# A decoder in float32r on one core: a weight tile's first part multiplied with both parts of x in one 512-column matmul

## The chip, the core and the metric

One of the cores of a Trainium2 chip runs the whole program. The metric is the device time of one execution in microseconds (us), the median of three runs. The engines are named as in the profile: PE is TensorE's matmuls, PEld its weight loads, DVE is VectorE, ACT is ScalarE, POOL is GpSimd, and SP issues DMAs.

## The reference, cut to what matters

256 tokens of width 1024 pass through five blocks in turn. Each has the same frame: a norm, weight matrices, a residual add.

```python
x = x + 0.5 * swiglu(rmsnorm(x, ff1_norm), w_gate, w_up, w_down)      # FF1, 1024 -> 2816 -> 1024
proj = rmsnorm(x, mix_norm) @ w_in                                    # mixer: 7168 columns
...                                                                   # gates, gMLP branch, stick-breaking attention
x = x + (g_a * (y_a @ w_branch_a) + g_b * (y_b @ w_branch_b)) @ w_out
x = x + 0.5 * swiglu(rmsnorm(x, ff2_norm), w_gate, w_up, w_down)      # FF2
h = rmsnorm(x, final_norm)                                            # the second network starts here
h = h + moba_attention(q, k, v) @ w_o_2[0];  h = h + relu(n(h) @ w_up)**2 @ w_down   # MLP a, 1024 -> 4096 -> 1024
h = h + forgetting_attention(q, k, v, c) @ w_o_2[1];  h = h + relu(n(h) @ w_up)**2 @ w_down   # MLP b
out = rmsnorm(h, final_norm_2)
```

All inputs are float32, and every weight element is used once for the 256 tokens.

## The kernel before, in words

**Split arithmetic.** A float32 product is made of three float32r matmuls. A weight W is split into a first part `whi` (W rounded to float32r, one ACT copy, line 130) and a rest `wlo` = W - `whi` (one DVE subtraction, line 137). The activations are split in the same way into `hnh` and `hnl`. The product is `whi·hnh + whi·hnl + wlo·hnh`.

**Stream of weights.** Weights come by DMA in 403 pieces of 128 x 1024 elements, called halves (`raw`, 6 buffers). Work is written out in units, mostly one half each. In unit u ACT splits half u+3 and DVE half u+2 (5 buffers of `whi`, 4 of `wlo`), then PE multiplies half u. A half holds 8 tiles of 128 x 128, so a unit is 24 matmuls. The loop at the end of the program sets the order of everything: for each unit the functions registered with `pre`, the two splits, those registered with `mid`, the unit's matmuls, and those registered with `at`. Each engine works through its own instructions in that order.

**Groups.** A `Group` is a pass over all rows of K for up to 1024 columns. The transposed output goes to PSUM: 128 columns of the weight on the partitions, 256 tokens along the bank, two such tiles to a bank of 512. A group of 1024 columns fills the four banks of one ring, "A" or "B", and the next group takes the other ring. After a group, DVE reads each bank with its next operation (times `rstd`, or the residual add), so there is no separate copy. Three kinds of groups work in another way: `v`, the mixer's `gv` and the last projection are token-major, with x as the stationary operand and 512 columns of weight moving.

**Norms.** `norm_at(u, ...)` is written into the first units of a block: sums of squares of x (ACT squares, DVE sums into `acc`), a matmul of `ones` with `acc` on PE (function `c`, at the end of unit u+3), a square root on ACT and a reciprocal on DVE (function `d`). The factor is applied when a group's banks are read, which is after 8 units.

**Residuals.** `resid` adds banks to `xT` on DVE and splits the new x for the next block: ACT writes the first part of each k-tile, DVE the rest. For two banks together it issues both adds, then the four first parts, then the four rests.

Of the kernel before, what the change touches and what calls it, by code (L numbers as in the profile page):

```python
# [15 lines left out]
D = 1024  # L16
# [10 lines left out]
class Group:  # L27
    """One pass over K of a weight matrix's columns, accumulating in two or four PSUM banks."""

    def __init__(self, ring, srcs, ktiles, xin, tok=False, stagger=0):  # L30
        self.ring, self.srcs, self.ktiles, self.xin = ring, srcs, ktiles, xin
        self.tok, self.stagger = tok, stagger
# [7 lines left out]
def decoder_kernel(  # L40
# [18 lines left out]
    psum = ctx.enter_context(tc.tile_pool(name="psum", bufs=4, space=bass.MemoryType.PSUM))  # L59
# [7 lines left out]

    def bank(ring):
        return psum.tile([128, 512], F32, name=f"ps{ring}", tag=f"ps{ring}")
# [10 lines left out]
    # ---------------------------------------------------------------- weight stream  # L80
# [59 lines left out]
    def unit_mm(u):  # L140
        g, hs = units[u]
        if g.ps is None:
            g.ps = [bank(g.ring) for _ in range(g.banks)]
            g.started = [False] * g.banks
# [6 lines left out]
        def ws(h, kl, b, parts=(0, 1, 2)):  # L151
            k = halves[h][1] + kl
            last = k == g.ktiles - 1
            for j in range(2):
# [3 lines left out]
                xh, xl = g.xin(k, nt)  # L158
                dst = g.ps[b][:, j * T:(j + 1) * T]
                for i in parts:  # L160
                    mm(b, dst, wl if i == 2 else wh, xl if i == 1 else xh, last and j == 1 and i == 2)

        def tsm(h, kl, tok, chs):
# [3 lines left out]
            xh, xl = g.xin(k, 0)  # L167
            xh, xl = xh[:, tok * 128:(tok + 1) * 128], xl[:, tok * 128:(tok + 1) * 128]
# [34 lines left out]
    # ---------------------------------------------------------------- constants  # L203
# [86 lines left out]
    # ---------------------------------------------------------------- norms  # L290
    def hn_tiles():
        return (big.tile([128, 8, T], F32R, name="hnh", tag="hnh"),
                big.tile([128, 8, T], F32R, name="hnl", tag="hnl"))

    def scaled(dst, src, cols, k):
        """dst = (hi, lo) of src times the per-partition gain; src is x^T's k-tile."""
        hh, hl = dst
        S.activation(hh[:, k, :], src, AF.Copy, scale=cols[:, k:k + 1])
        V.scalar_tensor_tensor(hl[:, k, :], src, cols[:, k:k + 1], raw32(hh[:, k, :]),
                               op0=OP.mult, op1=OP.subtract)  # L300
# [5 lines left out]
    def resid(g, alpha, outs, banks):  # L306
        """x^T += alpha * psum, then its scaled splits for the next layer."""
        for b in banks:
            xb = xT[:, 2 * b:2 * b + 2, :]
            V.scalar_tensor_tensor(xb, v2(g.ps[b]), alpha, xb, op0=OP.mult, op1=OP.add)  # L310
            for k in (2 * b, 2 * b + 1):
                for (hh, _), cols in outs:
                    S.activation(hh[:, k, :], xT[:, k, :], AF.Copy, scale=cols[:, k:k + 1])
        for b in banks:
            for k in (2 * b, 2 * b + 1):
                for (hh, hl), cols in outs:
                    V.scalar_tensor_tensor(hl[:, k, :], xT[:, k, :], cols[:, k:k + 1], raw32(hh[:, k, :]),
                                           op0=OP.mult, op1=OP.subtract)
# [3 lines left out]
    def squares(cols=None):  # L322
        sq = []
        for b in range(4):
# [10 lines left out]
    def add_up(acc, sq):  # L335
        V.tensor_add(sq[0], sq[0], sq[1])
        V.tensor_add(sq[2], sq[2], sq[3])
        V.tensor_add(sq[0], sq[0], sq[2])
        V.tensor_add(acc, sq[0][:, :T], sq[0][:, T:])

    def norm_at(u, ring, two=False, cols=False):
# [3 lines left out]
        def a():  # L345
            R.clear()
            R["sq"] = squares()
            R["acc"] = smalls.tile([128, 2, T], F32, name="acc", tag="acc", bufs=1)

        def b():  # L350
            add_up(R["acc"][:, 0, :], R["sq"])
            if two:
                R["sq"] = squares(gcol[:, G_FIN:G_FIN + 8])

        def b2():
            add_up(R["acc"][:, 1, :], R["sq"])

        def c():
            p = bank(ring)
            R["p"] = p  # L360
            PE.matmul(p[:, :n], ones, R["acc"].rearrange("p a t -> p (a t)")[:, :n], start=True, stop=True)
# [10 lines left out]
        def d2():  # L372
            """1 / sqrt(s2 / D + eps * (s1 / D + eps)): both norms' factors at once."""
            r = smalls.tile([128, T], F32, name="rstd2", tag="rstd", bufs=2)
            S.activation(r, R["p"][:, :T], AF.Copy, scale=EPS)
            V.tensor_add(r, r, R["p"][:, T:])
# [16 lines left out]
        def f():  # L393
            r = R["bc"]
            p = bank(ring)
# [5 lines left out]

        pre(u + 1, a)
        pre(u + 2, b)
        if two:
            pre(u + 3, b2)
        v = u + 4 if two else u + 3
# [14 lines left out]
    # ---------------------------------------------------------------- layers  # L421
# [3 lines left out]
    def hn_in(k, nt):  # L425
        return cur["hn"][0][:, k, :], cur["hn"][1][:, k, :]

    def fixed_in(name):
        def f(k, nt):
            h, l = cur[name]  # L430
            assert (id(h), k) in ready, (name, k)
            return h[k // 8][:, k % 8, :], l[k // 8][:, k % 8, :]
        return f
# [3 lines left out]
    def hidden(name, his, los):  # L437
        def mk():
            cur[name] = ([slot(i, [128, 8, T], F32R, name=name + "h") for i in his],
                         [slot(i, [128, 8, T], F32R, name=name + "l") for i in los])  # L440
        return mk

    def hid(name, nt):
        h, l = cur[name]
        return h[nt // 8][:, nt % 8:nt % 8 + 2, :], l[nt // 8][:, nt % 8:nt % 8 + 2, :]

    def put_hidden(u, name, nt, src, fin=None):
        """The split of two column tiles, its first part in unit u and its second in the next."""
        hv, lv = hid(name, nt)

        def lo():
            V.tensor_sub(lv, src, raw32(hv))
            ready.update((id(cur[name][0]), nt + j) for j in range(2))

        S.activation(hv, src, AF.Copy)
        pre(u + 1, lo)

    def swiglu_evac(u, g, n0, bg, bu, name):
        r = bc2(R["bc"])
        t, w = temp(name="gt"), temp(name="ut")  # L460
        tv, uv = v2(t[:, :512]), v2(w[:, :512])
        V.tensor_mul(tv, v2(g.ps[bg]), r)
        V.tensor_mul(uv, v2(g.ps[bu]), r)
        S.activation(tv, tv, AF.Silu)

        def b():
            V.tensor_mul(uv, uv, tv)
            put_hidden(u + 1, name, n0, uv)

        pre(u + 1, b)  # L470

    def ffn(ring, name, wg, wu, wd, his, los):
        other = {A: B, B: A}
        r, first = ring, None
        for i in range(6):
            c0 = 512 * i
            w = min(512, DFF - c0)
            g = add(Group(r, [(wg, c0, w), (wu, c0, w)], 8, hn_in))
            if first is None:
                first = g  # L480
                at(g.u0, hidden(name, his, los))
                norm_at(g.u0 or 2, other[r])
            nb = g.banks // 2
            for b in range(nb):
                at(g.u1 + b, swiglu_evac, g.u1 + b, g, 4 * i + 2 * b, b, nb + b, name)
            r = other[r]
        return add(Group(r, [(wd, 0, D)], DFF // 128, fixed_in(name), stagger=2))

    # start: x^T and its split
    g1, u1, d1 = ff1_w_gate[0], ff1_w_up[0], ff1_w_down[0]  # L490
    ff1 = ffn(A, "ffa", g1, u1, d1, (1, 2, 3), (4, 5, 6))

    def resid_to(g, alpha, bases):
        def f():
            outs = []
            cur["hn"] = hn_tiles()
            outs.append((cur["hn"], bases[0]()))
            if len(bases) > 1:
                cur["hn2"] = (slot(6, [128, 8, T], F32R, name="kvh"), slot(7, [128, 8, T], F32R, name="kvl"))
                outs.append((cur["hn2"], bases[1]()))  # L500
            resid(g, alpha, outs, (0, 1))
            at(g.u1 + 1, resid, g, alpha, outs, (2, 3))
        at(g.u1, f)
# [3 lines left out]
    # ---- mixer  # L507
    win = w_in[0]
    gates = [add(Group((B, A)[i], [(win, 5120 + i * D, D)], 8, hn_in)) for i in range(2)]
    norm_at(gates[0].u0, A, cols=True)  # L510
    at(gates[0].u0 + 1, late_consts)
    at(gates[0].u0 + 1, w_s_prep, A)
# [9 lines left out]
    def gate_evac(g, i, b):  # L522
        if b == 0:
            cur["gate", i] = slot((0, 7)[i], [128, 8, T], name="gate")
        t = temp(name="gl")
        V.tensor_mul(v2(t[:, :512]), v2(g.ps[b]), bc2(R["bc"]))
        for j in range(2):
            nt = 2 * b + j
# [669 lines left out]
```

## Time and profile before

| | |
|---|---|
| time, median of 3 runs | 1259.06 us (1258.83 to 1259.13) |
| profiled execution: span from its first to its last instruction | 1257.2 us |
| the same execution's own time | no separate figure is given; the median of the runs lies 1.9 us above the span |
| PE busy | 1247.9 us, 9770 instructions |
| DVE busy | 827.1 us |
| ACT busy | 663.5 us |
| mean granted clock of TensorE | 0.999 |
| DMA | 217.68 MB, mean 173 GB/s |

Busy time of an engine is the time in which at least one of its instructions is under way. Matmuls overlap in the pipeline, so what a matmul costs is read from the distance between the starts of two, not from its duration.

### The profile page before, as it was taken

To read this page: it belongs to the slowest core of one execution; us is meant where nothing else is said; L and a number is where in the kernel's file an instruction comes from. 1 tells how busy PE (TensorE), PEld (TensorE's weight loads), DVE (VectorE), ACT (ScalarE), POOL (GpSimd) and SP (SyncE) were. 2 spreads that over 40 slices of the span, in tenths; PEclk is the share of its full clock that TensorE was granted. 3 is DMA by queue.
4 is the path that set the end of the run, shared out by engine and by line. 5 is a ranking of instruction groups with operands and counts; after the bars stand their busy time and mean duration, and the time that the engine had idled before them with its cause. 6 is when DMAs were issued, how large, how long until landed. Compare 5 with 4: busy or idle time off the path is not lost.

```text
span 1257.2 us, 23928 instructions
## 1 busy us (share of the span) xinstructions
PE 1247.9 (99%) x9770; PEld 1197.9 (95%) x9770; DVE 827.1 (66%) x1226; ACT 663.5 (53%) x945; POOL 2.7 (0%) x7
## 2 busy tenths in 40 slices
PE   9999999999999999999999999999999999999997
PEld 8999999999989999999999899999999989999886
DVE  6765647658667676667568777755448677856644
ACT  6543436554666455444356655655336656655433
POOL 0000000000000000000000000000000000000000
PEclk9999999999999999999999999999999999999999
DMA  8665555755444456565555445655553434555661
GB/s 280 194 209 175 188 184 171 220 178 153 154 147 140 155 185 195 166 202 179 190 157 163 135 141 183 190 190 184 180 183 130 153 129 138 192 186 175 209 193 49
DMA packets 100095, 217.68 MB, mean 173 GB/s; under 512 B 10041, under 2 KB 39825, under 8 KB 99985
## 3 DMA queue, kind: packets, MB, share of 16 engines
q1 hardware_dynamic: 99408, 214.32, 53.1%
q10 hardware_dynamic: 576, 1.84, 0.4%
q8 instruction: 76, 1.25, 0.4%
q14 instruction: 35, 0.28, 0.1%
HBM read 215.07 MB, written 1.05 MB: 172 GB/s over the span
## 4 chain that ended last, share of the span: by engine, by line
PE 99%; DMA 0%; DVE 0%; SPq 0%; issue 0%; ACT 0%; POOL 0%; POOLq 0%
PE psB L148 49%; PE psA L148 43%; PE psB L693 1%; PE psB L673 1%; PE psA L693 1%; PE psA L735 0%; PE psA L673 0%; DMA xin<-in_x_dram 0%; PE psB L979 0%; PE psA L581 0%; PE psB L677 0%; PE psB L842 0%; PE psB L844 0%; PE psB L843 0%; PE psA L737 0%; PE psB L808 0%
## 5 line engine op out<-in xcount | busy, mean ns | idle before, releaser
L137 DVE TENSOR_TENSOR wlo<-raw,whi 128x1024 fp32r<-128x1024 f32 x403 | 488.2, 1221 | 243.9 <-PE psB L148 112.5
L130 ACT ACTIVATE whi<-raw 128x1024 fp32r<-128x1024 f32 x403 | 417.7, 1052 | 287.9 <-PE psB L148 171.2
L148 PE MATMUL psA<-hnh,whi 128*128 128x256 f32 x928 | 263.7, 286 | 0.0
L148 PE MATMUL psA<-hnh,wlo 128*128 128x256 f32 x928 | 261.4, 283 | 0.0
L148 PE MATMUL psA<-hnl,whi 128*128 128x256 f32 x928 | 261.2, 283 | 0.0
L148 PE MATMUL psB<-hnh,whi 128*128 128x256 f32 x800 | 228.1, 285 | 0.0
L148 PE MATMUL psB<-hnh,wlo 128*128 128x256 f32 x800 | 226.4, 283 | 0.0
L148 PE MATMUL psB<-hnl,whi 128*128 128x256 f32 x800 | 226.3, 283 | 0.0
L148 PEld LDWEIGHTS psA<-hnh,whi 128*128 128x128 f32 x928 | 177.4, 192 | 1.5 <-issue 1.1
L148 PEld LDWEIGHTS psA<-hnl,whi 128*128 128x128 f32 x928 | 177.5, 192 | 0.4 <-issue 0.2
L148 PEld LDWEIGHTS psA<-hnh,wlo 128*128 128x128 f32 x928 | 177.4, 192 | 0.2 <-DVE wlo L137 0.2
L148 PEld LDWEIGHTS psB<-hnh,whi 128*128 128x128 f32 x800 | 153.5, 192 | 0.5 <-issue 0.3
L148 PEld LDWEIGHTS psB<-hnl,whi 128*128 128x128 f32 x800 | 153.5, 192 | 0.1
L148 PEld LDWEIGHTS psB<-hnh,wlo 128*128 128x128 f32 x800 | 153.5, 192 | 0.0
L148 PE MATMUL psB<-mah,whi 128*128 128x256 f32 x256 | 72.4, 283 | 0.0
L148 PE MATMUL psB<-mal,whi 128*128 128x256 f32 x256 | 72.4, 283 | 0.0
L148 PE MATMUL psB<-mah,wlo 128*128 128x256 f32 x256 | 72.4, 283 | 0.0
L148 PE MATMUL psB<-whi,mbh 128*128 128x512 f32 x128 | 49.9, 390 | 0.0
L148 PE MATMUL psB<-wlo,mbh 128*128 128x512 f32 x128 | 49.8, 389 | 0.0
L148 PE MATMUL psA<-ffah,whi 128*128 128x256 f32 x176 | 49.8, 283 | 0.0
L148 PE MATMUL psA<-ffal,whi 128*128 128x256 f32 x176 | 49.8, 283 | 0.0
L148 PE MATMUL psA<-ffah,wlo 128*128 128x256 f32 x176 | 49.8, 283 | 0.0
(305 smaller groups left out, 2264.9 us busy)
## 6 DMA issues: line engine op xcount, KB each, us to landing
raw<-in_w_up_dram SPq DMA_DIRECT2D x64, 512.0 KB, 4.2
raw<-in_w_down_dram SPq DMA_DIRECT2D x64, 512.0 KB, 3.5
raw<-in_ff_w_gate_dram SPq DMA_DIRECT2D x88, 256.0 KB, 3.2
raw<-in_ff_w_up_dram SPq DMA_DIRECT2D x88, 256.0 KB, 4.2
raw<-in_ff_w_down_dram SPq DMA_DIRECT2D x44, 512.0 KB, 4.0
raw<-in_w_in_dram SPq DMA_DIRECT2D x40, 512.0 KB, 4.2
raw<-in_w_in_dram SPq DMA_DIRECT2D x32, 256.0 KB, 3.0
raw<-in_moba_w_qkv_dram SPq DMA_DIRECT2D x32, 256.0 KB, 3.0
```

The costliest lines, as they stand in the source:

```text
L130: S.activation(hi_t[h], raw_t[h].rearrange("p k c -> p (k c)"), AF.Copy)
L137: V.tensor_sub(lo_t[h], raw_t.pop(h).rearrange("p k c -> p (k c)"), raw32(hi_t[h]))
L148: PE.matmul(dst, lhsT, rhs, start=not g.started[b], stop=stop, skip_group_check=True)
L673: PE.matmul(O[64 * h:64 * h + 64, 0:256], vv[:, 0, c:c + 64], w[:, h * 384:h * 384 + 256], start=True, stop=False, skip_group_check=True)
L693: PE.matmul(banks[h][:, c:c + n], left[i][rw, cl:cl + 128], right[j][rw, cr:cr + n], start=start and i + j == 0, stop=i == 1, skip_group_c ...
```

## The change

A group may now be `wide`. In a wide group a bank belongs to one tile of 128 columns. Its left half (256 tokens) takes `wlo·xh` and `whi·xh`, its right half takes `whi·xl`. Since the two parts of x lie next to each other now (one tile `[128, k, 2, T]` in place of two tiles), `whi` meets both in one matmul of 512 columns. Reading needs the sum of the two halves: `gather` copies the right halves of two banks to SBUF on ACT and adds the left halves on DVE. A wide group has 512 columns, so it is 4 units and not 8. Wide are the two feed-forward blocks, the gates, `u`, `w_out`, and both MLPs with their down projections except the last one: 2080 tiles, of which the first 16 run in three matmuls of 256 columns, as before.

With this go: PSUM tiles of two banks (`banks2`, two to a ring), the norm's functions one unit earlier (`c` at the end of unit u+2) and in two halves, `resid` one pair of banks at a time, and the attention biases of MoBA made at the start of FF2 and not in its down projection.

```diff
-        self.banks = self.width // 256
+        self.banks = self.width // (128 if wide else 256)
...
-    psum = ctx.enter_context(tc.tile_pool(name="psum", bufs=4, space=bass.MemoryType.PSUM))
+    psum = ctx.enter_context(tc.tile_pool(name="psum", bufs=2, space=bass.MemoryType.PSUM))
...
+            if g.wide:
+                col = kl * g.width + b * 128
+                wh, wl = hi_t[h][:, col:col + 128], lo_t[h][:, col:col + 128]
+                x = g.xin(k, b)
+                if len(parts) == 3:
+                    mm(b, g.ps[b][:, :T], wl, x[:, 0, :], False)
+                    mm(b, g.ps[b], wh, both(x), last)
...
+    def gather(g, p, name="gs"):
+
+        t = v2(temp(name=name)[:, :512])
+        S.activation(t, g.pairs[p][:, :, T:], AF.Copy)
+        V.tensor_add(t, g.pairs[p][:, :, :T], t)
+        return t
+
+    def resid(g, p, n0, alpha, outs):
+
+        xb = xT[:, n0:n0 + 2, :]
+        if g.wide:
+            t = v2(temp(name="rs")[:, :512])
+            S.activation(t, g.pairs[p][:, :, T:], AF.Copy)
+            V.scalar_tensor_tensor(xb, t, alpha, xb, op0=OP.mult, op1=OP.add)
+            src = g.pairs[p][:, :, :T]
+        else:
+            src = v2(g.ps[p])
+        V.scalar_tensor_tensor(xb, src, alpha, xb, op0=OP.mult, op1=OP.add)
+        for k in (n0, n0 + 1):
+            for ts, cols in outs:
+                S.activation(part(ts, k, 0), xT[:, k, :], AF.Copy, scale=cols[:, k:k + 1])
+        for k in (n0, n0 + 1):
+            for ts, cols in outs:
+                V.scalar_tensor_tensor(part(ts, k, 1), xT[:, k, :], cols[:, k:k + 1], raw32(part(ts, k, 0)),
+                                       op0=OP.mult, op1=OP.subtract)
...
-        pre(u + 1, a)
-        pre(u + 2, b)
-        if two:
-            pre(u + 3, b2)
-        v = u + 4 if two else u + 3
+        pre(u if u0 is None else u0, a0)
+        pre(u + 1, a1)
+        mid(u + 1, b)
+        v = u + 3 if two else u + 2
         at(v, c)
...
-        for i in range(4):
-            g = add(Group(r, [(w, D * i, D)], 8, hn_in))
+        for i in range(8):
+            g = add(Group(r, [(w, 512 * i, 512)], 8, hn_in, wide=True))
...
+            def evac(g=g, i=i, p=0):
+                tv = gather(g, p, "rl")
+                V.scalar_tensor_tensor(tv, tv, 0.0, bc2(R["bc"]), op0=OP.max, op1=OP.mult)
                 S.activation(tv, tv, AF.Square)
-                pre(g.u1 + b + 1, put_hidden, g.u1 + b + 1, name, 8 * i + 2 * b, tv)
+                pre(g.u1 + p + 1, put_hidden, g.u1 + p + 1, name, 4 * i + 2 * p, tv)
...
+    def down(r, w, ktiles, xin, stagger=2):
+
+        return [add(Group((r, flip(r))[i], [(w, 512 * i, 512)], ktiles, xin, stagger=i * stagger, wide=True))
+                for i in range(2)]
...
-        at(ff2.u0 + 1 + h, moba_bias, h)
+        at(ff2[0].u0 - 43 + h, moba_bias, h)
```

**PE, two weight tiles in FF1.** Before, three matmuls of 256 columns to a tile:

```order
L148 MATMUL psB<-hnh,whi 128x256
L148 MATMUL psB<-hnl,whi 128x256
L148 MATMUL psB<-hnh,wlo 128x256
L148 MATMUL psB<-hnh,whi 128x256
L148 MATMUL psB<-hnl,whi 128x256
L148 MATMUL psB<-hnh,wlo 128x256
```

and now, three tiles of the same block (`hn` holds both parts of x):

```order
L161 MATMUL psB<-hn,wlo 128x256
L161 MATMUL psB<-hn,whi 128x512
L161 MATMUL psB<-hn,wlo 128x256
L161 MATMUL psB<-hn,whi 128x512
L161 MATMUL psB<-hn,wlo 128x256
L161 MATMUL psB<-hn,whi 128x512
```

The matmul with `wlo` stands first now, and the one with `hnl` is gone as an instruction of its own.

**DVE at the start of MLP a.** `xT` rows are residual adds, `hnl` (now `hn`) the rests of the split x, `sq` and `acc` the norm's sums, `wlo` the splits of the weight stream, `rstd` the reciprocal. Before:

```order
L137 TENSOR_TENSOR wlo<-raw,whi 128x1024
L310 SCALAR_TENSOR_TENSOR xT<-psA,xT 128x512 x2
L317 SCALAR_TENSOR_TENSOR hnl<-xT,gcol,hnh 128x256 x4
L137 TENSOR_TENSOR wlo<-raw,whi 128x1024
L336 TENSOR_TENSOR sq<-sq 128x512
L337 TENSOR_TENSOR sq<-sq 128x512
L338 TENSOR_TENSOR sq<-sq 128x512
L339 TENSOR_TENSOR acc<-sq 128x256
L137 TENSOR_TENSOR wlo<-raw,whi 128x1024 x2
L368 RECIPROCAL rstd<-rstd 128x256
```

and now, from the first sum of squares on:

```order
L383 TENSOR_TENSOR sq<-sq 128x512
L149 TENSOR_TENSOR wlo<-raw,whi 128x1024
L348 SCALAR_TENSOR_TENSOR xT<-psA,xT 128x512
L354 SCALAR_TENSOR_TENSOR hn<-xT,gcol,hn 128x256 x2
L348 SCALAR_TENSOR_TENSOR xT<-psA,xT 128x512
L354 SCALAR_TENSOR_TENSOR hn<-xT,gcol,hn 128x256 x2
L149 TENSOR_TENSOR wlo<-raw,whi 128x1024
L391 TENSOR_TENSOR sq<-sq 128x512
L392 TENSOR_TENSOR sq<-sq 128x512
L393 TENSOR_TENSOR acc<-sq 128x256
L149 TENSOR_TENSOR wlo<-raw,whi 128x1024
L405 RECIPROCAL rstd<-rstd 128x256
```

Each add is now followed by its own two rests, one sum has moved ahead of the second pair of adds, and between `acc` and the reciprocal stands one `wlo` and not two.

**DVE between two groups of MLP a.** `rl` is the tile that holds relu of the group's columns, `mal` (now `ma`) the rest of the hidden activations. Before:

```order
L892 SCALAR_TENSOR_TENSOR rl<-psB,rstd 128x512
L137 TENSOR_TENSOR wlo<-raw,whi 128x1024
L892 SCALAR_TENSOR_TENSOR rl<-psB,rstd 128x512
L452 TENSOR_TENSOR mal_8935<-rl,mah_8931 128x512
L137 TENSOR_TENSOR wlo<-raw,whi 128x1024
L892 SCALAR_TENSOR_TENSOR rl<-psB,rstd 128x512
L452 TENSOR_TENSOR mal_8935<-rl,mah_8931 128x512
```

and now, all of one group's cycle:

```order
L335 TENSOR_TENSOR rl<-psB,rl 128x512
L945 SCALAR_TENSOR_TENSOR rl<-rl,rstd 128x512
L149 TENSOR_TENSOR wlo<-raw,whi 128x1024
L335 TENSOR_TENSOR rl<-psB,rl 128x512
L945 SCALAR_TENSOR_TENSOR rl<-rl,rstd 128x512
L483 TENSOR_TENSOR ma_7743<-rl,ma_7743 128x2x256
L149 TENSOR_TENSOR wlo<-raw,whi 128x1024
L483 TENSOR_TENSOR ma_7743<-rl,ma_7743 128x2x256
L149 TENSOR_TENSOR wlo<-raw,whi 128x1024 x2
```

Each pair of tiles has one DVE operation more (line 335, the sum of the two halves), and it stands behind an ACT copy. The cycle comes every 4 units and not every 8.

## Rows read from the trace of the kernel before

**Rows 1.** The page: busy time, granted clock in 40 slices, chain that ended last.

```profile
PE 1247.9 (99%) x9770; PEld 1197.9 (95%) x9770; DVE 827.1 (66%) x1226; ACT 663.5 (53%) x945; POOL 2.7 (0%) x7
...
PEclk9999999999999999999999999999999999999999
...
PE 99%; DMA 0%; DVE 0%; SPq 0%; issue 0%; ACT 0%; POOL 0%; POOLq 0%
```

**Rows 2.** The chain in order of time: start, duration, engine, tile, line, count.

```profile
136.80 63.36 PE psA L148 x528
...
1182.78 68.03 PE psB L148 x300
```

**Rows 3.** Timeline, PE: two matmuls of 512 columns; one of 384 and its successor.

```profile
1200.31 0.39 PE L148 MATMUL psB<-whi,mbh 128*128 128x512 f32 x1
1200.54 0.39 PE L148 MATMUL psB<-wlo,mbh 128*128 128x512 f32 x1
...
336.61 0.34 PE L735 MATMUL psA<-spl,tri 128*128 128x384 f32 x1
336.78 0.22 PE L737 MATMUL psA<-sph,nones 128*128 128x128 f32 x1
```

**Rows 4.** Groups by line and shape: busy us, mean ns of one, idle before.

```profile
L137 DVE TENSOR_TENSOR wlo<-raw,whi 128x1024 fp32r<-128x1024 f32 x403 | 488.2, 1221 | 243.9 <-PE psB L148 112.5 <-PE psA L148 75.5 <-issue 28.3
L130 ACT ACTIVATE whi<-raw 128x1024 fp32r<-128x1024 f32 x403 | 417.7, 1052 | 287.9 <-PE psB L148 171.2 <-PE psA L148 95.8 <-ACT whi L130 9.2
L893 ACT ACTIVATE rl<-rl 128x512 f32<-128x512 f32 x32 | 20.0, 624 | 27.1 <-DVE rl L892 27.1
L313 ACT ACTIVATE hnh<-xT,gcol 128x256 fp32r<-128x256 f32 x40 | 17.9, 499 | 15.4 <-DVE xT L310 15.4
L982 ACT ACTIVATE ncb<-psB 128x512 f32<-128x512 f32 x8 | 4.3, 596 | 4.3 <-PE psB L979 4.3
```

**Rows 5.** Windows, FF1 and MoBA attention: length, busy PE, PEld, DVE, ACT, POOL; clock; DMA share, GB/s.

```profile
40.00:130.00 90.00, 90.00 (x752) 90.00 (x751) 56.20 (x63) 40.38 (x47) 0.00 (x0) 1.00 0.58 187
680.00:760.00 80.00, 80.00 (x635) 70.98 (x634) 62.10 (x175) 48.52 (x112) 0.00 (x0) 1.00 0.45 144
```

**Rows 6.** Timeline, DVE and ACT, start of MLP a (first unit at 763.39).

```profile
760.36 1.28 DVE L310 SCALAR_TENSOR_TENSOR xT<-psA,xT 128x512 f32<-128x512 f32 x2
...
764.35 1.28 DVE L310 SCALAR_TENSOR_TENSOR xT<-psA,xT 128x512 f32<-128x512 f32 x2
...
768.36 0.69 DVE L336 TENSOR_TENSOR sq<-sq 128x512 f32<-128x512 f32 x1
768.96 0.68 DVE L337 TENSOR_TENSOR sq<-sq 128x512 f32<-128x512 f32 x1
...
770.40 0.43 DVE L339 TENSOR_TENSOR acc<-sq 128x256 f32<-128x256 f32 x1
...
765.07 1.71 ACT L313 ACTIVATE hnh<-xT,gcol 128x256 fp32r<-128x256 f32 x4 [1.34 <-DVE xT L310]
766.69 2.18 ACT L327 ACTIVATE sq<-xT 128x512 f32<-128x512 f32 x4
```

**Rows 7.** The chain in order of time, start of MLP a.

```profile
763.39 11.52 PE psB L148 x96
774.91 0.43 PE psA L361 x2
```

**Rows 8.** Timeline, DVE, start of the FoX layer and of the mixer.

```profile
950.41 1.22 DVE L928 CAST sel<-ident 128x2048 fp32r<-128x2048 f32 x1
...
204.64 0.22 DVE L270 CAST identb<-ident 128x128 bf16<-128x128 f32 x1
...
207.57 0.69 DVE L336 TENSOR_TENSOR sq<-sq 128x512 f32<-128x512 f32 x1
```

**Rows 9.** Timeline, DVE, the mixer's layer norm (first and last rows).

```profile
273.22 0.42 DVE L557 BATCH_NORM_STATS2 st<-gv 128x6 f32<-128x256 f32 x1
...
290.95 1.22 DVE L137 TENSOR_TENSOR wlo<-raw,whi 128x1024 fp32r<-128x1024 f32 x1
```

More of the change, by code (lines that the diff above doesn't have):

```diff
@@ L142, in unit_mm @@
         if g.ps is None:
-            g.ps = [bank(g.ring) for _ in range(g.banks)]
+            g.pairs = [banks2(g.ring) for _ in range(g.banks // 2)]
+            g.ps = [t[:, i, :] for t in g.pairs for i in range(2)]
             g.started = [False] * g.banks
@@ L288, in w_s_prep, with hn_tile, part, xpair @@
         V.memset(wmT[64:128, :, 0:64], 0.0)
[L291 to L300, printed above, removed]
+    def hn_tile():
+        return [big.tile([128, 8, 2, T], F32R, name="hn", tag="hn")]
+    def part(ts, k, i, n=1):
+        per = 8 // len(ts) if len(ts) == 1 else 4
+        v = ts[k // per][:, k % per:k % per + n, i, :]
+        return v if n > 1 else v[:, 0, :]
+    def xpair(ts, k):
+        per = 8 // len(ts) if len(ts) == 1 else 4
+        return ts[k // per][:, k % per]
     def split(hi, lo, src):
@@ L304, in split, with squares @@
         V.tensor_sub(lo, src, raw32(hi))
[L306 to L318, printed above, removed]
+    def gather(g, p, name="gs"):
[20 more added lines that the diff above has]
+                                       op0=OP.mult, op1=OP.subtract)
     R = {}
-    def squares(cols=None):
+    def squares(half, cols=None):
         sq = []
-        for b in range(4):
+        for b in (2 * half, 2 * half + 1):
             t = temp(name="sq")
@@ L360, in c @@
             R["p"] = p
-            PE.matmul(p[:, :n], ones, R["acc"].rearrange("p a t -> p (a t)")[:, :n], start=True, stop=True)
+            PE.matmul(p[:, :n], ones, both(R["acc"])[:, :n], start=True, stop=True)
             r = smalls.tile([128, T], F32, name="rstd", tag="rstd", bufs=2)
@@ L394, in f @@
             r = R["bc"]
-            p = bank(ring)
+            p = bank(fring or ring)
             for t in range(2):
@@ L472, in ffn @@
-    def ffn(ring, name, wg, wu, wd, his, los):
-        other = {A: B, B: A}
+    def ffn(ring, name, wg, wu, wd, slots):
         r, first = ring, None
[L475 to L478, printed above, removed]
+        for i in range(DFF // 256):
+            g = add(Group(r, [(wg, 256 * i, 256), (wu, 256 * i, 256)], 8, hn_in, wide=True))
             if first is None:
                 first = g
[L481 to L487, printed above, removed]
@@ L508, in decoder_kernel @@
     win = w_in[0]
-    gates = [add(Group((B, A)[i], [(win, 5120 + i * D, D)], 8, hn_in)) for i in range(2)]
-    norm_at(gates[0].u0, A, cols=True)
+    r = flip(ff1[1].ring)
+    gates = []
+    for i in range(4):
+        gates.append(add(Group(r, [(win, 5120 + i * 512, 512)], 8, hn_in, wide=True)))
+        r = flip(r)
+    norm_at(gates[0].u0, flip(gates[0].ring), cols=True, fring=gates[0].ring)
     at(gates[0].u0 + 1, late_consts)
-    at(gates[0].u0 + 1, w_s_prep, A)
+    at(gates[0].u0 + 1, w_s_prep, flip(gates[0].ring))
@@ L591, in spatial_evac @@
         V.tensor_mul(v2(t[:, :512]), v2(t[:, :512]), cur["u"][:, 2 * b:2 * b + 2, :])
-        yh, yl = (y[:, 2 * b:2 * b + 2, :] for y in cur["ya"])
+        yh, yl = (part(cur["ya"], 2 * b, i, 2) for i in range(2))
         S.activation(yh, v2(t[:, :512]), AF.Copy)
@@ L913, in decoder_kernel @@
+    qs, vs = qkv_groups(r, wqkv, 0, wqkv, D, wqkv, 2 * D, hn_in, (1, 7), 0, wait=7)
+    norm_at(qs[0].u0, flip(r), two=True, cols=True)
+    at(qs[0].u1, hidden("oa", (8, 5)))
+    wo = add(Group(r, [(w_o_2[0], 0, D)], 8, fixed_in("oa"), stagger=2))
+    soft_attention(qs, vs, flip(r), "oa", moba_terms, 8)
+    resid_to([wo], 1.0, [lambda: colsof(G_MLP)])
+    r = mlp(flip(r), "ma", w_up_2[0], (2, 3, 4, 0, 1, 6, 7, 5))
+    dn = down(r, w_down_2[0], 32, fixed_in("ma"))
     resid_to(dn, 1.0, [lambda: colsof(G_AT, 1), lambda: colsof(G_KV)])
@@ L931, in fox_f1 @@
         wf = fx["wf"]
-        p = bank(B)
+        p = bank(FP)
         for k in range(8):
-            h, l = kv_in(k, 0)
+            h, l = (kv_in(k, 0)[:, i, :] for i in range(2))
             PE.matmul(p[:, :T], wf[:, 0, k, :], h, start=k == 0, stop=False, skip_group_check=True)
@@ L1076, in decoder_kernel @@
     S.preload_act_table(AF.Copy)
-    p = bank(A)
-    warm = bank(A)
+    warm2 = banks2(A)
+    p, warm = warm2[:, 0, :], warm2[:, 1, :]
     def warm_up(n):
@@ L1095, in first_half @@
         w = raw_t.pop(0)
-        parts = [slice(i * 256, i * 256 + 256) for i in range(g.banks)]
+        parts = [slice(i * 128, i * 128 + 128) for i in range(g.banks)]
         return ([lambda c=c: S.activation(wh[:, :, c], w[:, :, c], AF.Copy) for c in parts],
```

303 lines of the change are left out of this document (161 added, 142 removed).

## The prediction

> **What bounds the kernel now.** I read the page first: PE is busy for 99% of the span at full clock, and the chain that ended last is PE for 99% [rows 1]. A busy PE can still hide waits, so next the chain in order of time: 528 matmuls of 256 columns take 63.36 us, which is 120.0 ns from start to start, without a gap, and whole blocks repeat that number [rows 2]. PE has no wait worth a term; the kernel is bound by the number and width of its matmuls. DVE and ACT are busy for 62% and 45% of FF1, and DMA for 58% [rows 5]. Their idle time ends at PE: `wlo` and `whi` wait for a buffer that PE gives back [rows 4].
>
> **What a matmul costs.** 300 matmuls of 512 columns take 68.03 us, 226.8 ns each [rows 2]; the timeline shows the same distance, 0.23, and 0.17 for 384 columns [rows 3]. From 256 to 512 columns the distance grows by 106.8 ns, which is 256 columns at 2.4 GHz. So 13.2 ns of each matmul do not depend on its columns; 384 columns should then take 173 ns, and they do. A tile costs 3 x 120.0 = 360 ns now. In a wide group it is 120.0 + 226.8 = 346.8: the columns stay, one matmul goes. The order shows 2064 such tiles (the first 16 keep three matmuls), so PE loses 2064 x 13.2 = 27.2 us. No row shows a 256-column matmul behind one of 512 columns; the bounds are 0, if the pair took 360, and 27.2. I take 27.2, since the same sum holds inside streams of either width.
>
> The Trainium skill speaks against this much: TensorE: Matmul & The Clock Gate, in the section on 56 against 53.3 ns, gives a fixed cost of about 2.5 ns per warm matmul. By it the change would save an estimated 5 us. This case's rows give 13.2, and the measurement decides.
>
> **What reading costs.** Each pair of tiles gets one ACT copy (596 ns for 512 elements out of PSUM [rows 4]) and one DVE add (0.69). There are 104 such pairs, so about 62 us of ACT and 72 of DVE, both off the path unless a `wlo` comes late. Where that could be is seen in MLP a, whose cycle of 4 units x 8 tiles x 346.8 = 11.1 us is the tightest. Take as 0 the start of the next group's first matmul. From [rows 4, 6] I use: a hand-over to another engine 0.04 (ACT starts at 765.07 behind an add that began at 764.35 and lasts 0.69); DVE's next operation 0.60 behind one of 0.69, or 0.72 where it reads the result (768.96 to 770.40 is two such steps); on ACT the next starts some 0.1 before the last ends (1.71 for four of 499 ns). The first two banks end two tiles early, so the copy runs from -0.49 to 0.11. Then: add 0.15, times `rstd` 0.87, square 1.59, first part 2.25, `whi` 2.79, second copy 3.74 to 4.34, add 4.38, times `rstd` 5.10, rest 5.70, `wlo` 6.30 to 7.52. That `wlo` is for the unit that starts at 3 x 2.774 = 8.32, and its weight load goes one matmul (0.12) and a hand-over ahead: 0.64 us to spare. FF1 and FF2 have no second ACT operation in the chain and some 1.2 to spare. Cost in these blocks: 0. If this cover goes, each group pays the excess.
>
> **What the joints between blocks cost.** Here the change moves work up against its deadline. The norm's matmul `c` stands at the end of unit u+3 now (774.91, that is 11.52 behind the first unit at 763.39 [rows 7]). DVE finishes `acc` at 770.83 [rows 6], 4.1 us ahead of it. In the changed kernel `c` comes after three units of 2.774, at 8.32, and PE does nothing while it waits for `acc`. The sums get later too. Counted from 763.39, DVE gets to the first residual add at -3.03 [rows 6]. One pair of banks at a time, DVE waits for ACT's first parts between its add and its rests: add 0.69, hand-over, two first parts of 0.50 some 0.40 apart [rows 4, 6], the last rest: 2.08 to the next add. So adds at -3.03 and -0.95, last rest to 1.21. ACT's two squares end at 1.76, the first sum runs from 1.80, `wlo` from 2.40, adds at 3.55 and 5.63, `wlo` from 7.71, and the three sums from 8.85, 9.57 and 10.29, done at 10.72. PE stands still from 8.32 to about 10.75: **2.4 us**. `d` and the next `wlo` then follow with room, because PE is late by as much. MLP b has the same order: 2.4 again.
>
> The other joints go by the same sum, with what is particular to each:
> - FF1: x and weights arrive as before; four squares and two copies of x stand ahead of the sums: `c` waits 1.7.
> - Mixer: `c` waits 0.4 behind four transposes; then the masks and constants (204.64 to 207.57, 2.9 us of DVE [rows 8]) stand between `acc` and the `wlo` of unit u+4, which has only a unit to spare: 1.3 more. Together 1.7.
> - `u` of the gMLP: two gathers, some 2.8 us of DVE, fall into the layer norm, where DVE runs nearly without a pause (273.22 to 290.95 [rows 9]), with deadlines 0.11 us earlier each unit. What was spare is gone: 2.0 (bounds 0 and 3.5).
> - FF2: 0.8 for `c`, 0.2 for the biases made there: 1.0.
> - MoBA: two norms at once, `wlo` of unit u+3 late by 0.5, `c` by 0.6 and the next `wlo` by 0.3: 1.4.
> - FoX: each first part and rest is made twice, for two norms, and the cast to `sel` (1.22 [rows 8]) stands ahead of the sums, so `acc` is done at 12.0 where three units of 2.88 end at 8.64: 3.4.
>
> The sum is 1.7 + 1.7 + 2.0 + 1.0 + 1.4 + 2.4 + 3.4 + 2.4 = **16.0 us**. The bounds are 0, if DVE gets to these adds earlier than I let it, and about twice as much, if what comes late at a joint also delays the next `wlo`.
>
> **What costs nothing.** DMA: the rows of a weight piece shrink to 1 KB in FF1 and FF2, but the MoBA windows, whose q and k pieces have such rows, move 144 GB/s at a share of 0.45 and FF1 187 at 0.58 [rows 5]; both make some 320 GB/s of a whole share. PSUM in pairs: a ring's pairs are read by 5.1 in the cycle above, and the ring is wanted again at 11.1.
>
> **Sum.** The profiled execution's span is 1257.2. 1257.2 - 27.2 + 16.0 = 1246.0; the median of the runs shown lies 1.9 above the span, so 1247.9.
>
> **Rivals.**
> - **The joints are covered.** DVE is idle for a third of FF1, and all joints have work that could go ahead. Against it: engines keep the written order, and the sums stand behind the rests. It gives 1257.2 - 27.2 + 1.9 = 1231.9. Chance 0.15.
> - **The joints cost nearly double**, some 25 us: a late `c` puts the reciprocal behind it, and the first reading with it. It gives 1257, between 1253 and 1260. Against it: after `c` waits, PE's deadlines move as well. Chance 0.16.
> - **Slower: the cycle of reading becomes the bound.** If the chain from copy to `wlo` is longer than my sum, every group of the MLPs (16) pays the excess over 0.64 and every one of FF1 and FF2 (22) that over 1.2. The remaining gain of 11.2 is gone when 16 (y - 0.64) + 22 (y - 1.2) = 11.2, at y = 1.25 us. With 1.6 it is 16 x 0.96 + 22 x 0.4 = 24 us, a time of 1272. For it: three hand-overs between engines per pair, and two-bank reads that no row shows. Against it: 1.25 us is a sixth of the chain. Chance 0.08.
> - **The change doesn't do what it says:** a 512-column matmul behind one of 256 columns costs what the two did before, and the joints remain: 1257.2 + 16.0 + 1.9 = 1275. Against it stand two equal constants from 256, 384 and 512 columns. Chance 0.03. By the Trainium skill's 2.5 ns (TensorE: Matmul & The Clock Gate, the section on 56 against 53.3 ns) it would be an estimated 1270.
>
> **How the numbers follow.** The forecast holds 0.58, with a range of its own from 1242 to 1253. The range for 8 in 10 reaches down to the covered joints and up to the lower part of the doubled ones: 1232 to 1257. A measurement of this kernel tells about 0.2% (2.5 us) from no change, so faster is below 1256.5: the forecast, the covered joints and two thirds of the doubled ones, 0.58 + 0.15 + 0.10 = 0.83. Within 0.2%: 0.06. Slower: 0.08 + 0.03, 0.11.
>
> **What would show it.** In the changed profile 528 matmuls of a down projection become 352, in 61.0 us. PE's idle time, near zero within groups, appears before `c` (the matmul of `ones`) at seven places, longest in FoX, and ahead of some `wlo` in the mixer. Within MLP a the groups are 11.1 us apart; more than 11.2 shows the cycle as a bound. The forecast is wrong if a wide tile takes 360 ns, if `c` waits for nothing, or if PE waits for `wlo` in every group.

## The result and the profile after

The changed kernel takes 1293.12 us (1288.72 to 1295.46, 4 runs) against 1259.1 us (1258.83 to 1259.78, 4 runs) for the kernel before: a ratio of 1.0266, with a 95% interval from 1.0247 to 1.0284. It is slower. 1247.9 had been forecast, with a range that ended at 1257.

The page of its profiled execution (1292.58 us), to be read beside [rows 1]:

```profile
span 1290.8 us, 19769 instructions
...
PE 1241.7 (96%) x7706; PEld 1091.0 (85%) x7706; DVE 897.9 (70%) x1328; ACT 712.3 (55%) x1049; POOL 2.7 (0%) x7
...
PE 83%; DVE 10%; ACT 4%; issue 2%; DMA 1%; SPq 0%; DVEq 0%; POOL 0%; ACTq 0%; POOLq 0%
```

2064 matmuls are gone, and PE is busy for 6 us less. But the chain that ended last, which was PE for 99% of the time, now runs through DVE and ACT for 14%: PE waits. The chain in order of time shows both halves of this, beside [rows 2, 7] (start, length, what, how often):

```profile
37.21 11.09 PE psA L161 x64
...
601.19 30.51 PE psA L161 x176
...
786.22 0.88 DVE hn L354 x2
787.11 1.14 DVE wlo L149
788.24 0.61 DVE sq L391
788.88 0.70 DVE sq L392
789.60 0.43 DVE acc L393
790.04 0.14 issue
790.17 0.67 PE psA L398 x2
790.84 4.35 PE psB L161 x16
795.19 11.30 PE psA L161 x64
806.49 11.31 PE psB L161 x64
```

In these groups the forecast is met to the digit: 88 wide tiles take 30.51 us, 346.7 ns each, and a group of four units 11.09. At the joint to MLP a PE waits for `acc`, as foreseen. Behind it 16 matmuls take 4.35 us where 2.77 would do, and the groups 11.30; both are taken up at the end. So who is waited for? The waits of PE, longest first in total (who waited for whom: us in total, times, longest):

```profile
PE psA L398 <- DVE acc L393: 6.8, 4, 3.5
PE psA L863 <- DVE mx L866: 5.9, 8, 0.7
PE psB L788 <- ACT sw L792: 5.3, 8, 1.2
PE psB L759 <- DVE za L760: 5.2, 8, 0.7
PE psA L161 <- DVE wlo L149: 3.8, 4, 1.8
PE psB L398 <- DVE acc L393: 3.7, 3, 2.5
PE psA L1036 <- ACT ncb L1039: 3.4, 4, 1.4
PE psB L1164 <- DVE hn L1178: 2.4, 2, 2.2
PE psA L161 <- ACT qk L666: 1.4, 1, 1.4
```

Before, PE's waits were 3.0 us in all:

```profile
PE psA L1083 <- DVE ident L209: 1.4, 1, 1.4
PE psB L1105 <- DMA xin<-in_x_dram: 1.3, 2, 0.7
PE psB L148 <- DVE gate L763: 0.3, 1, 0.3
```

Two kinds stand in the changed kernel. `acc` and `qk` are at the joints that the prediction spoke of (`qk` at MoBA's, which it has, though not with this wait). Of the 3.8 us of `wlo` only 0.8 are, at the gates; 1.8 lie at `w_out` and 1.2 in MLP a's down projection, where it has nothing. Four of the rows are inside attentions, L863, L788, L759 and L1036, the first three eight times each: once for each pair of heads. L1164 is the turning of x at the start. No step of the prediction has these five. One pair in the mixer's attention, PE alone:

```profile
379.81 0.34 PE L788 MATMUL psB<-sph,tri 128*128 128x384 f32 x1
379.99 0.34 PE L788 MATMUL psB<-spl,tri 128*128 128x384 f32 x1
380.17 0.22 PE L790 MATMUL psB<-sph,nones 128*128 128x128 f32 x1
380.23 0.27 PE L790 MATMUL psB<-spl,nones 128*128 128x128 f32 x1
381.08 0.44 PE L788 MATMUL psB<-sph,tri 128*128 128x384 f32 x1 [0.58 <-ACT sw L792]
...
382.64 0.28 PE L759 MATMUL psB<-maskS,identb 128*128 128x256 bf16 x1
383.57 0.27 PE L759 MATMUL psB<-maskS,identb 128*128 128x256 bf16 x1 [0.65 <-DVE za L760]
```

The first head's four matmuls end, ACT takes the exponential of that head's bank (`sw`, 0.49 us), and only then does PE begin on the second head, whose bank nobody reads. From 380.23 to 381.08 PE starts nothing. The same happens between the two mask matmuls, 0.93 us apart. Before, the second head's matmul came 0.10 us behind the first head's last, and the two mask matmuls stood together:

```profile
371.94 0.27 PE L737 MATMUL psA<-spl,nones 128*128 128x128 f32 x1
372.04 0.39 PE L735 MATMUL psA<-sph,tri 128*128 128x384 f32 x1
...
373.55 0.39 PE L706 MATMUL psA<-maskS,identb 128*128 128x256 bf16 x2
```

Two banks are one PSUM tile now. The built programs show it without a time. In the kernel before, PE's first matmul with `tri` for the second head (L735) waits for no other engine, and DVE's copy of the second head's bank in the other attentions (L846) waits for PE, which writes that bank. In the changed kernel both (L788, L901) wait for ACT, which has touched the other bank of the same tile.

### The profile page after: what moved, and what is told of

Its sections match the earlier page's. It is cut to its first block, busy times and chain, and to the rows that moved or that the text cites. A ratio compares the mean times of both kernels' runs of the same rounds, so it can differ in the third digit from the quotient of the medians.

```text
span 1290.8 us, 19769 instructions
## 1 busy us (share of the span) xinstructions
PE 1241.7 (96%) x7706; PEld 1091.0 (85%) x7706; DVE 897.9 (70%) x1328; ACT 712.3 (55%) x1049; POOL 2.7 (0%) x7
## 4 chain that ended last, share of the span: by engine, by line
PE 83%; DVE 10%; ACT 4%; issue 2%; DMA 1%; SPq 0%; DVEq 0%; POOL 0%; ACTq 0%; POOLq 0%
PE psA L161 45%; PE psB L161 32%; DVE wlo L149 3%; PE psB L745 1%; DVE xT L348 1%; DVE hn L354 1%; ACT hn L351 1%; PE psB L725 1%; PE psB L788 1%; DVE xT L344 1%; ACT sq L364 0%; DMA raw<-in_ff_w_up_dram 0%; DVE sq L392 0%; ACT whi L142 0%; DVE za L760 0%
## 5 line engine op out<-in xcount | busy, mean ns | idle before, releaser
L161 PE MATMUL psA<-hn,whi 128*128 128x512 f32 (+1 forms) x1232 | 342.7, 347 | 0.0
L161 PE MATMUL psB<-hn,whi 128*128 128x512 f32 (+1 forms) x832 | 273.3, 379 | 0.0
L161 PE MATMUL psA<-hn,wlo 128*128 128x256 f32 x960 | 270.1, 283 | 0.9 <-DVE wlo L149 0.8
L161 PEld LDWEIGHTS psA<-hn,whi 128*128 128x128 f32 x1232 | 213.7, 190 | 33.9 <-issue 3.8
L161 PE MATMUL psB<-hn,wlo 128*128 128x256 f32 x768 | 217.2, 283 | 0.8 <-DVE wlo L149 0.8
L161 PEld LDWEIGHTS psA<-hn,wlo 128*128 128x128 f32 x960 | 182.3, 190 | 2.7 <-DVE wlo L149 1.8
L161 PEld LDWEIGHTS psB<-hn,whi 128*128 128x128 f32 x832 | 152.5, 189 | 34.2 <-issue 4.0
L161 PEld LDWEIGHTS psB<-hn,wlo 128*128 128x128 f32 x768 | 145.8, 190 | 1.4 <-DVE wlo L149 1.1
L161 PE MATMUL psA<-whi,mb 128*128 128x512 f32 x256 | 79.2, 389 | 0.0
L161 PE MATMUL psA<-wlo,mb 128*128 128x512 f32 x128 | 49.8, 389 | 0.0
```

Source lines behind the costliest of these rows:

```text
L161: PE.matmul(dst, lhsT, rhs, start=not g.started[b], stop=stop, skip_group_check=True)
```

## The experiments

**Theory P**: the shared tile makes PE wait for the reader of the other bank. **Theory J**: the joints cost about twice what was forecast, and the attentions only pass their lateness on. **Theory C**: the merged matmul, or reading two banks at once, costs more than forecast. In each edit "-" is the changed kernel unless said otherwise.

**Matmuls of both banks ahead of the reads** (and both turnings of x ahead of the first read). One of five places:

```diff
         for h in range(2):
             PE.matmul(v2(hb[h])[:, :, 0:128], identb, maskS, start=False, stop=True, skip_group_check=True)
+        for h in range(2):
             V.tensor_scalar(a[:, h * 384:h * 384 + 384], hb[h][:, :384], 30.0, None, op0=OP.min)
```

> The changed kernel with its two-bank PSUM tiles, but the matmuls of both halves of a tile stand ahead of the reads of either half, at four places: the mask matmuls of both attentions that have them, the sums of the stick-breaking attention, FoX's gate sums, and the turning of x at the start. Theory P (two banks in one tile let PE wait for the reader of the other bank): the waits that the changed kernel's trace shows there go, 8 x 0.82 + 0.6 and 8 x 0.81 in the mixer, 8 x 0.81 and 4.1 in FoX, 2.4 at the start, 26.7 us in all, so about 1266 us; PE's wait for the exponential of the first head, for its clipped scores and for FoX's maxima is gone. Theory J (sums of squares and rests that come late at the joints cost about twice what was forecast, and the waits inside the attentions only pass this lateness on): 1285 to 1293. Theory C (a wide pair of matmuls or the reading of two banks at once costs more than forecast): 1293, within 0.2%.

Measured: 1265.2 us (1264.89 to 1267.53), ratio to before 1.0053 [1.0038, 1.0068]. No wait is left in the pairs:

```profile
372.98 0.27 PE L791 MATMUL psB<-spl,nones 128*128 128x128 f32 x1
373.09 0.39 PE L789 MATMUL psB<-sph,tri 128*128 128x384 f32 x1
...
374.60 0.39 PE L759 MATMUL psB<-maskS,identb 128*128 128x256 bf16 x2
```

28 us come back by moving instructions that do the same work, 26 of them in the two attentions. J and C fall as the main cause. The turning of x gained nothing: FF1's first part took 129.43 us against 128.94.

**The kernel before with two-bank tiles alone** ("-" is the kernel before; the same at each place that takes banks):

```diff
-            g.ps = [bank(g.ring) for _ in range(g.banks)]
+            g.pairs = [banks2(g.ring) for _ in range(g.banks // 2)]
+            g.ps = [t[:, i, :] for t in g.pairs for i in range(2)]
...
-        hb = [bank(ring), bank(ring)]
+        hb = banks2(ring)
+        hb = [hb[:, 0, :], hb[:, 1, :]]
```

> The kernel before with two-bank PSUM tiles alone: every pair of banks is one tile, nothing else is changed (256-column matmuls, groups of 1024 columns, norms and residuals as before). Theory P: the same waits appear in the mixer's attention and in FoX as in the changed kernel, 13.7 and 10.6 us, and up to 2 at the start: 1283 to 1286 us. Theory J or C: no more than 1262, since neither the joints nor the matmuls are touched.

Measured: 1287.53 us (1287.01 to 1288.86), 28.5 more than before. The waits are those of the changed kernel, to the tenth:

```profile
PE psB L815 <- DVE mx L818: 5.9, 8, 0.7
PE psA L741 <- ACT sw L745: 5.3, 8, 1.2
PE psA L712 <- DVE za L713: 5.2, 8, 0.7
PE psB L987 <- ACT ncb L990: 3.4, 4, 1.4
```

**The merged matmul split again:**

```diff
-                    mm(b, g.ps[b], wh, both(x), last)
+                    mm(b, g.ps[b][:, :T], wh, x[:, 0, :], False)
+                    mm(b, g.ps[b][:, T:], wh, x[:, 1, :], last)
```

> The changed kernel with the 512-column matmul of each wide tile made as two of 256 columns, into the same two halves of the bank; nothing else. If the merged matmul is worth 13.2 ns in each of 2064 tiles whatever else waits, PE loses 27.2 us more: 1320 us, and a down projection's 176 tiles take 63.4 us again. Theory C (the merge is worth less than forecast, or the wide matmul itself makes others wait): under 1310. If PE's waits were elsewhere so long that they hide it, also under 1310.

Measured: 1310.96 us (1310.0 to 1312.7), 17.8 more and not 27.2. The down projections of FF1 and FF2 took 63.36 us each again, so the price of a tile is back; where PE waits at a joint, slower matmuls only shorten the wait. This run left open whether the rest was hidden or not there; the run with the joints mended, below, takes it up.

**The norm's matmul of ones one unit later** (and the first group of a block read one unit later), on top of the first experiment:

```diff
-        v = u + 3 if two else u + 2
+        v = u + 4 if two else u + (3 if u0 is None else 2)
```

> As the first kernel of this set, and the norm's matmul of ones one unit later in every block but FF1 (at the end of unit u+3, in MoBA u+4, as in the kernel before), with the first group of a block read one unit later. If the joints' stalls are that matmul's wait for the sums, the waits seen in the changed kernel go with it (gates 0.4, FF2 1.0, MoBA 0.9, MLP a 2.6, FoX 3.7, MLP b 2.6: 11.2 us), so about 11 us below the first kernel. If the lateness is in the rests and in the weights' second parts that follow, the wait moves on to these, and the gain is under 4 us.

Measured: 1261.53 us (1256.61 to 1263.86): 3.7 less, by the total the second expectation (under 4), by stage some of each. In FoX the stall is gone (the first two groups take 26.55 us, as before), while FF1's first part takes 1.8 more (131.21 against 129.43). In MLP a and b it is not: PE now waits for `wlo` of units 2 to 4, and the block takes 92.35 us against 92.06. There the lateness sits in the rests and second parts, and only its last member had been the sums.

**Five places at the joints** (FF1's first group copied out before its factor is known, masks made in FF1's down projection, layer norm a unit later, biases back in FF2's down projection, a pair of each down projection read a unit later), on top of that; two of the five:

```diff
-    at(gates[0].u0 + 1, late_consts)
+    at(ff1[0].u0 + 3, late_consts)
...
-        at(ff2[0].u0 - 43 + h, moba_bias, h)
+        at(ff2[0].u0 + 1 + h + (h > 8), moba_bias, h)
```

> As the run with the norm one unit later, and five more places mended where PE still waits in its trace: FF1's first group is copied out of PSUM before its factor is known, so that the matmul of ones can come at unit 5 (waits of 2.1 and, in part, 2.4 at the start); the masks are made in FF1's down projection and not among the gates (1.9); four pieces of the layer norm stand a unit later (1.0); MoBA's biases are made in FF2's down projection (0.5 of 1.2); the second pair of a first half of a down projection is read a unit later (2.2 at w_out, 0.5 each at FF1, FF2 and MLP a's 1.4). If the joints are a matter of where DVE's work stands, about 8 us come back: 1253, and faster than the kernel before. If the stalls only move to the next weight's second part, as part of them did in the run before, 1258 to 1261.

Measured: 1250.35 us (1248.4 to 1251.61), ratio 0.9926 [0.991, 0.9943]: 11 us back, faster than before. At the joints it is in the main a matter of where DVE's work stands; the five were changed together, and no run tells them apart.

**The order of the two matmuls of a tile**, on top of that: the 512 columns first.

> The same with the two matmuls of a wide tile in the other order: the 512-column matmul of the first part ahead of the 256-column one of the rest. The trace of the changed kernel has stretches in which a unit of 8 wide tiles takes 2.774 us and others in which it takes 2.827, with the same code and no wait between; the slower ones begin and end at stalls or at the same units of a block. If the order in the tile (which matmul follows a semaphore or a change of bank) decides it, the slower stretches go or all become slow: a difference of up to 5 us either way, seen in the down projections' units. If it is something else, the same share of units is slow and the time within 2 us.

Measured: 1247.0 us (1246.55 to 1252.95). Of the wide units that run without a wait, 77 are slow (2.827) and 157 fast (2.774), against 145 and 83. But the ranges of the two kernels overlap, and the slow stretches still begin and end at stalls. Inconclusive; the last run settles more.

**One-bank tiles, everything else as in the changed kernel** (here `gather`; the same at each place that takes or reads banks):

```diff
-        S.activation(t, g.pairs[p][:, :, T:], AF.Copy)
-        V.tensor_add(t, g.pairs[p][:, :, :T], t)
+        for i in range(2):
+            S.activation(t[:, i, :], g.ps[2 * p + i][:, T:], AF.Copy)
+        for i in range(2):
+            V.tensor_add(t[:, i, :], g.ps[2 * p + i][:, :T], t[:, i, :])
```

> The changed kernel with PSUM tiles of one bank again (four to a ring) and the order of its instructions kept; what reads two banks at once reads each by itself, in operations of 256 elements (a pair is gathered by two ACT copies and two DVE adds, and a residual pair takes one operation more on each engine). Theory P in its plain form (it is the shared tile that makes PE wait, not the order and not the bank): the waits in the mixer's attention, in FoX and at the start go without any reordering, 26 us, and the attentions' stages take what they took before. The smaller readings cost some 0.3 us more on ACT and 0.15 on DVE per pair; if the cover in the groups holds, about 1266, if it doesn't, up to 1275. If it is the order of the matmuls and reads itself that costs, 1290.

Measured: 1254.95 us (1252.31 to 1257.66), ratio 0.9965 [0.9953, 0.9977]. This one edit takes 38 us off the changed kernel and makes it faster than before. The order of matmuls and reads is the changed kernel's, and all waits in the attentions are gone; what is left is the joints:

```profile
PE psA L398 <- DVE acc L393: 4.9, 2, 2.6
PE psB L398 <- DVE acc L393: 4.0, 3, 2.3
PE psA L157 <- DVE wlo L146: 2.1, 3, 1.0
```

It was below the lowest expectation: by the table below it gains at the joints, `w_out` and the end too. The cover in the groups held although reading takes more operations: the groups still take 11.09 us.

**The norm's sums a unit later**, on top of the version with the 512 columns first (`mid(u + 2, b)` for `mid(u + 1, b)`):

> The best version so far (joints mended, 512-column matmul first in a tile), and the norm's three last sums a unit later, behind the next weight's second part. In that version PE waits at MLP a and MLP b about 1.5 us each for second parts of weights in units 2 to 4, and 2.1 at MoBA. If the sums ahead of these delay them, 3 to 5 us come back: 1243. If they are late because of the rests ahead, nothing changes, or the matmul of ones waits again: 1246 to 1250.

Measured: 1251.06 us (1245.26 to 1252.25): nothing gained. PE's waits for `wlo` fall from 2.8 to 1.4 us, and it waits 2.6 for `acc` again: the wait only changes its name.

**The split with the joints mended:**

> The best version so far (joints mended, 512-column matmul first in a tile), with that matmul split into two of 256 columns. The split of the changed kernel itself cost 17.8 us and not 27.2. If the rest was hidden under PE's waits at the joints and in the attentions, which are mostly gone here, the split costs close to 27 us: 1272 to 1274, a little less by what the slower stretches of the unsplit kernel cost (77 units by 0.05, 4 us): from 1270. If the merge is worth only some 18 us for another reason, 1265.

Measured: 1265.96 us (1265.92 to 1266.16), 19.0 more and not 27: the figure of the second expectation. (The unsplit kernel's four runs reach up to 1252.95, so the figure is uncertain by some us.) By stage the split costs 4.25 of 4.65 us in FF2's first part, 2.35 of 2.32 in its down projection, 3.41 of 3.38 in MLP a's; but 1.2 of 4.65 and 1.17 of 2.32 in FF1, where 56 of the unsplit kernel's slow units lie, and 2.4 of 3.4 in each MLP's first part. So the 13.2 ns are right where nothing else changes, and some 8 of 27 us are not seen in the total: nearly half for the slow units, and the rest, it seems, for waits that become shorter.

**What helped, together**, with one-bank tiles:

> What helped, together: one-bank tiles with the order of the changed kernel, the norm one unit later, the five places of the joints, the 512-column matmul first in a tile. Against the best version so far, with two-bank tiles (1247.0), the last stage is 1.3 us shorter with one-bank tiles, the mixer's third branch 0.7 to 1.0 and FF1's first part 0.6 to 0.8, and w_out is up to 1.3 longer: 1245, if the parts add up; not under 1241. If the smaller readings now come late at the joints, 1250.

Measured: 1241.93 us (1241.47 to 1242.77), ratio 0.9864 [0.9848, 0.9881]; 3 less than the parts add up to.

**All wide matmuls of a unit first:**

```diff
-            for h, kl in seq:
-                for b in range(g.banks):
-                    ws(h, kl, b)
+            for parts in ((0, 1), (1, 2)) if g.wide else ((0, 1, 2),):
+                for h, kl in seq:
+                    for b in range(g.banks):
+                        ws(h, kl, b, parts)
```

> The same, and in each unit of a wide group all eight 512-column matmuls first and then all eight of 256 columns, so that the widths change twice a unit and not sixteen times, and the second part of a weight is wanted 1.8 us later. If the stretches with 2.827 us for a unit come from the change of width from matmul to matmul, they go, and the runs of one kernel lie closer together; if the joints' last waits are for second parts of weights, these shrink too: 1238 to 1241. If the slower stretches have another cause, they stay with about the same share of units, and only the second parts' slack is gained: 1242 to 1245.

Measured: 1242.19 us (1242.11 to 1242.22). The slow stretches go, but so do the fast ones: nearly all units take 2.79 us.

```profile
576.72 30.73 PE psA L157 x176
```

30.73 us for 88 tiles lies between the 30.51 of a fast stretch and the 31.1 that a slow one would take (11.30 for 32 tiles), and the total is the same. So the two speeds go with the alternation of widths, in the one profiled execution that each kernel has.

## Why the prediction was wrong

The span grew by 33.6 us; it had been forecast to shrink by 11.2. The table takes each stage's length, from its first weight matmul to the next stage's, and subtracts the length before less 13.2 ns for each of the 2064 tiles that lose a matmul. What remains is what the change added (us): PE's waits, and what a lower clock and a slower rhythm (both below) cost.

| stage | forecast | changed | reads behind both matmuls | one-bank tiles | one-bank, joints mended |
|---|---|---|---|---|---|
| FF1, first part | 1.7 | 5.0 | 5.5 | 3.2 | 3.4 |
| gates | 1.7 | 2.7 | 2.7 | 1.4 | 0.7 |
| `u` of the gMLP | 2.0 | 1.4 | 1.4 | 1.0 | 0.4 |
| mixer's attention and branches | 0 | 15.8 | 1.3 | 0.5 | 0.0 |
| `w_out` | 0 | 3.3 | 4.8 | 1.7 | 0.4 |
| FF2, first part | 1.0 | 1.3 | 1.0 | 0.4 | 0.2 |
| MoBA, first two groups | 1.4 | 2.8 | 2.8 | 1.5 | 1.3 |
| MoBA, the rest | 0 | 0.0 | 0.0 | 0.0 | 0.0 |
| MLP a, first part | 2.4 | 5.9 | 2.9 | 4.2 | 1.1 |
| FoX, first two groups | 3.4 | 3.7 | 6.3 | 4.3 | 0.0 |
| FoX, the rest | 0 | 11.6 | 0.0 | 0.0 | 0.0 |
| MLP b, first part | 2.4 | 2.9 | 2.9 | 2.7 | 2.2 |
| down projections, end | 0 | 4.7 | 4.6 | 1.6 | 1.1 |
| sum | 16.0 | 61.1 | 36.1 | 22.6 | 10.8 |

The changed column is 45.1 above the forecast: 27.4 in the mixer and FoX behind their first groups, 9.7 at the eight joints that had a term, 8.0 at `w_out`, the down projections and the end.

- **The matmul term was right in most stretches, and a little too large in sum.** 13.2 ns a tile is seen in the fast stretches without waits, some 140 units in the changed kernel; some 80 others, also without a wait, run at 2.827 us a unit, 353.4 ns a tile, where half of the 13.2 is left. By the Trainium skill's 2.5 ns per matmul (TensorE: Matmul & The Clock Gate, the section on 56 against 53.3 ns) the merge would have saved an estimated 0.4 us in the 176 tiles of FF2's down projection; it saved 2.35 (63.36 us with the split, 61.01 without).
- **Reading was hidden**, as forecast: PE waits within no group of the MLPs. MLP a's groups are 11.30 apart, which the prediction would have read as the cycle being the bound ("more than 11.2"); it is the slower rhythm instead, and MLP b's are 11.09.
- **"PSUM in pairs: a ring's pairs are read by 5.1 in the cycle above, and the ring is wanted again at 11.1" is the step that failed.** It asked only when a pair comes free for the next group, in the MLPs. It did not ask what within a pair waits for what, and the attentions, whose code changes only in how it takes its banks, got no term at all. There PE and a reader take turns on the two banks, and each turn now waits: 27.4 us in the mixer and FoX, of which 26.1 went when the matmuls were moved ahead of the reads. (About 1.4 of them are a stretch at the lower clock behind one such wait: 12 matmuls at 355.21 take 4.20 us, where 12 at 1003.44 take 2.77.) MoBA is the control. It uses the same tiles, but has no mask matmul between the reads, so PE is done with both banks before anyone reads, and its rest costs 0.0. Two-bank tiles alone put 28.5 us on the kernel before; one-bank tiles take 38 off the changed one. What that gains beyond the attentions, some 11 us, lies at the joints, `w_out` and the end; there a pair is read by two engines in turn, but no run separates this from the other effects of the edit.
- **The joints were right in place, and for one-bank tiles nearly right in sum.** PE waits for `acc` at seven places, longest in FoX, as foretold. In MLP b `acc` was forecast to be done 10.72 us behind the block's start; it was after 10.97 (1112.96 less 1101.99). FoX's matmul of ones waited 3.65 for 3.4. With one-bank tiles the eight joints sum to 18.7 against 16.0, and some 3 of that is the lower clock, 1.6 each in MLP a and FoX. In the changed kernel itself they sum to 25.7, about what the rival of nearly doubled joints gave. FF1 was not right in its parts: in the changed kernel `c` waited 0.5 there for 1.7, and the turning of x 2.4, which had no term. Missed were `w_out` and, as the code reads, that FF1 wants all of x within four units, where groups of 1024 columns had given it eight; no run tests the latter alone.
- **The slow rival was the wrong one.** "The cycle of reading becomes the bound" did not happen. The rival that was missing stood in the waits of the built program.
- **The range** let the joints vary and nothing else, so it could not reach a cost in stages without a term.

That a stalled PE also lost clock made MLP a worse (below): of its 5.9 some 2.6 are the wait for `acc`, 1.6 the clock and 1.5 the seven slower groups.

## What to carry to other kernels

When a change makes one tile out of two buffers, list every place where one engine writes one part while another reads the other: here each such turn became a wait, and the waits of the built program name it before any run. They don't tell its price: DVE's copy waits for ACT in MoBA too, and PE loses nothing there. The Trainium skill (Perfetto Trace Analysis, Optimization Strategy, on consistent bubbles) says that a gap that repeats on the engine that should be saturated can mean too little room for the next tile; the trace has such gaps, eight times at each of three places in the mixer and FoX, but the room was the same eight banks, and what counted was that two of them were one tile. A saving on the bound engine was worth its full price only in stretches where that engine waited for nothing and kept its faster rhythm: in both pairs of kernels a third of 27 us did not reach the total.

## What was not expected of the hardware

**Two speeds of alternating widths.** With 256 and 512 columns in turn, a unit of 8 tiles takes 2.774 us in some stretches and 2.827 in others, without any wait: 11.09 against 11.30 us a group. The speed changes at stalls and at a few fixed units. With the widths sorted neither is left, and nearly all units take 2.79. The cause in PE stays open.

**The clock after a stall.** In the windows view (length, busy time of the engines, granted clock, DMA share):

```profile
787.00:791.00 4.00, 1.53 (x8) 1.13 (x8) 3.93 (x6) 3.92 (x6) 0.00 (x0) 1.00 0.36 113
791.70:795.10 3.40, 3.40 (x12) 2.83 (x11) 3.04 (x3) 1.20 (x2) 0.00 (x0) 0.50 0.46 154
...
973.90:977.60 3.70, 0.31 (x3) 0.11 (x1) 3.63 (x6) 2.01 (x3) 0.00 (x0) 1.00 0.10 32
977.70:990.00 12.30, 12.30 (x101) 12.25 (x102) 8.60 (x11) 7.56 (x10) 0.00 (x0) 1.00 0.62 203
```

Behind the stall at MLP a PE runs for 3.4 us at the lower level, 1.2 GHz; that is the 4.35 us for 16 matmuls, 1.6 lost. Behind a longer stall at FoX it doesn't. The changed kernel has three such stretches before its last microseconds (from 16.8, 354.8 and 791.7), the version with one-bank tiles and mended joints none: a stall can cost more than its length, but not each does.
